# First projection and values of a hybrid encoder layer: scaled fp16 pairs for rounded-fp32 pairs, and values in 512 columns

## The chip, the core and the metric

The program runs on one core of a Trainium2 chip. The metric is the device time of one execution in microseconds; a version's time is the median of its runs. TensorE is called PE below, its weight loads PEld, VectorE DVE, ScalarE ACT, GpSimd POOL and SyncE SP. Hi and lo are the two halves of a pair that stands for one fp32 number: hi is the number in a shorter format, lo is what is left of it.

## What is computed

The layer works on 2048 tokens of 1024 features. The part that the change touches is its first line and what reads it:

```python
y = rmsnorm(h, norm_mix_g[l]) @ w_in[l]                 # (2048, 1024) @ (1024, 2560)
q = partial_rotary(y[..., 0:D_ATT].reshape(B, S, ATT_HEADS, HEAD_DIM))          # 512 columns
k = partial_rotary(y[..., D_ATT:2 * D_ATT].reshape(B, S, ATT_HEADS, HEAD_DIM))  # 512
v = y[..., 2 * D_ATT:3 * D_ATT].reshape(B, S, ATT_HEADS, HEAD_DIM)              # 512
att = dilated_sliding_attention(q, k, v).reshape(B, S, D_ATT)
c0 = 3 * D_ATT
conv = conformer_conv(y[..., c0:c0 + D_CONV], y[..., c0 + D_CONV:c0 + 2 * D_CONV],   # a, g
                      conv_w[l], conv_b[l], conv_ln_g[l], conv_ln_b[l])
h = h + jnp.concatenate([att, conv], axis=-1) @ w_out[l]
```

`conformer_conv` begins with `a * sigmoid(g)` and a convolution of 31 taps over the tokens. A cross-attention to 256 memory tokens and an MLP follow; the change doesn't touch them. The gain `norm_mix_g` lies around 5.7 here, and the weights are of the order of 1/32.

## The kernel before

**Layout and products.** The activations are kept feature-major: 8 tiles of 128 features (`KC`), 4 groups of 512 tokens (n = 0 to 3). Each product of the layer that needs fp32 accuracy is three matmuls (`mm3`, L201 to L204): hi by hi (L202), hi by lo and lo by hi (L203, L204), all in rounded fp32 (fp32r). A weight tile is 8 x 128 rows of 128 output columns. ACT makes its hi (L193), POOL or DVE its lo (L194), in `wsplit2`.

**Stages up to the first attention.** `setup0` and `setup` transpose the gains into `gv` and the convolution's weights into `cw` (times 0.5). `memory` projects the memory and forms two products of weights, which go to `ascr` and `bscr`; it uses the tiles of token groups 2 and 3 as scratch. Woven into it, `xprep` loads x, transposes it on PE (tile xt, L336), stores x^T to `xscr`, multiplies by gain and rms on DVE and splits the result into `XH_` (ACT) and `XL_` (POOL).

The projection follows as a row of units, one for each weight tile, run by `pipeline` (L494): the unit that computes is followed by one whose weights are being split and one whose weights are being loaded. The row is glu 0, glu 1 (each a unit g and a unit a, for token groups 0 and 1), eight units of keys and queries (`lin_qk`; kr and qr hold the rotary rows, gathered with strides), then glu 2, values 0, glu 3, values 1. Each tile of 512 tokens takes 24 matmuls into the PSUM tile `lin`. ACT takes the tanh of g, and DVE forms `u = (tanh + 1) * a`, which goes to `uscr`.

`lin_v` turns the operands round: a tile of 128 tokens of x is the stationary operand and 256 weight columns move, so a unit has 16 tiles of tokens of 24 matmuls each (tile v) into `vtok`, as an fp16 pair. `vscale` first works out a power of two for each value column (tile vsq: squares on ACT, sums on POOL and PE, the power on POOL and a bit mask on DVE). `lin_v` broadcasts it over the partitions (tile vbc, a transpose on PE) and multiplies the raw weights by it (L575). Its inverse, `vinv`, is applied after the attention. `edges` fills the first and last 256 rows of `vtok` from a tile of zeros, `zrow`, which is one of the two buffers of the tag raw.

**Beside it.** The convolution's 31 steps per tile (L219, DVE) are woven into the units. During the first attention, `rest` (L1118) weaves in glu 0 to 3 for token groups 2 and 3 in fine steps, each unit with its weights loaded and split again; then two tiles of `w_out` are fetched ahead.

**What sets the order.** Within each engine instructions run in the order in which the program's scheduler put them; it follows the order of the code and its own time line. Nearly all DMAs are issued by one queue, SP, in order, and one whose buffer isn't free yet holds those behind it. Raw weight tiles have two buffers, and so have their halves.

Of the kernel before, what the change touches and what calls it, by code (L numbers as in the profile page):

```python
# [10 lines left out]
F32 = mybir.dt.float32  # L11
# [10 lines left out]
P = 128  # L22
# [25 lines left out]
def hybrid_layer(ctx, tc, A, out):  # L48
# [12 lines left out]
    top.tile([P, 304], F32, name="tpad")  # L61
# [78 lines left out]
    cst.tile([P, 48], F32, name="cpad")  # L140
    lin = ExitStack()
# [7 lines left out]
    def setup():  # L149
# [14 lines left out]
        ACT.activation(cw.rearrange("p a b -> p (a b)"), pv[:, 64:192], AF.Copy, scale=0.5)  # L164

# [49 lines left out]
    def conv_unit(c, n, alloc, u):  # L215
        acc = alloc("acc", (P, 512), f"cacc{c}_{n}")
        DVE.tensor_scalar(acc, u[:, 0:512], cw[:, c, 0:1], gain("conv_b", c), op0=ALU.mult, op1=ALU.add)
        for t in range(1, CW):
            DVE.scalar_tensor_tensor(acc, u[:, t:t + 512], cw[:, c, t:t + 1], acc, op0=ALU.mult, op1=ALU.add)  # L219
            if t % 4 == 0:  # L220
                yield
# [62 lines left out]
    lp = pool("lin", stack=lin)  # L284
    xna.update({n: pool(f"x{n}", stack=early, side="right") for n in (0, 1)})
# [3 lines left out]
    def xpool(part, i, n, name, shape=(P, 2, 512), dtype=F32R):  # L289
        return xna[n].tile(list(shape), dtype, tag=f"x{part}{i}", name=name)  # L290
# [33 lines left out]
    def xprep(sp, n):  # L324
# [8 lines left out]
        for k in range(KC):  # L333
# [7 lines left out]
            DVE.scalar_tensor_tensor(xv, pt, gain("mix", k), rbs, op0=ALU.mult, op1=ALU.mult)  # L341
            ACT.copy(XH_[k, n], xv)
            POOL.tensor_tensor(XL_[k, n], xv, f(XH_[k, n]), op=ALU.subtract)
# [6 lines left out]
    def memory(sp):  # L350
        nat = [load_nat(sp, A["mem"][0, P * j:P * (j + 1), :], f"mn{j}") for j in range(2)]
        mh, ml = ([xpool(q, i, 3, f"m{q}{i}", (P, 4, NMEM)) for i in range(2)] for q in "hl")
# [22 lines left out]
        def wtiles(name, shape=(P, 8, P)):  # L375
            i = cnt[0] % 4
            cnt[0] += 1
            if i < 2:
                return [wp.tile(list(shape), dt, tag=t, name=f"m{t}_{name}", bufs=2)
                        for t, dt in (("raw", F32), ("whi", F32R), ("wlo", F32R))]  # L380
            return [xpool(q, j, 2, f"m{q}{j}_{name}", shape, dt)
                    for q, j, dt in (("h", i - 2, F32), ("h", i, F32R), ("l", i, F32R))]
# [21 lines left out]
        def ttiles(name):  # L404
            return [[xpool(q, 2 + i, 3, f"t{q}{name}{i}", (P, 4, NMEM)) for i in range(2)] for q in "hl"]
# [88 lines left out]
    def pipeline(*units):  # L494

        next(units[0])
        next(units[0])
        if len(units) > 1:
            next(units[1])
        for i, u in enumerate(units):  # L500
            if i + 1 < len(units):
                next(units[i + 1])
# [1303 lines left out]
```

## Time and profile before

| | |
|---|---|
| time, median of 3 runs | 2836.22 us (2830.67 to 2845.19) |
| profiled execution: time | 2833.89 us |
| profiled execution: span of the trace | 2832.1 us |
| mean granted clock of PE | 0.991 |
| matmuls in the trace | 15148 |
| bytes moved | 552.00 MB, 195 GB/s over the span |

The profile is one execution. Its span goes from the first to the last recorded instruction; 1.8 us of the execution lie outside it. Busy times are sums per engine over the span. In the views of groups a row has the count, the sum and the mean of one instruction, then the idle time of its engine just before them and what ended it. In a timeline a row has the start in us, the duration, the engine, the line, the operation, and output <- inputs with their shape. Matmuls are pipelined, so the duration of one is longer than the distance to the next. The chain of waits is read from top to bottom in order of time; a row has its start, its length and the work that ended last there.

### The profile page before, as it was taken

Reading aid. Unit: us, or ns where it says so; the run is one execution under the profiler, and the core shown is the slowest. Engines: PE = TensorE matmul, PEld = TensorE weight load, DVE = VectorE, ACT = ScalarE, POOL = GpSimd, SP = SyncE. Lnnn points to the kernel's source line nnn. Section 1 sums busy time; section 2 is a strip of 40 time slices with the busy share of each in tenths; the row PEclk is TensorE's granted clock in tenths of the full one; section 3 lists DMA queues with packets and bytes.
Section 4 is the critical chain, followed back from the end, with each engine's and each line's share of the span. In section 5 each row is a group of like instructions: output and inputs, shape, how many; then the busy total and the mean of one; then the engine's idle time right before and its main releaser. Section 6 shows DMA issues by size and latency. Waiting matters only on the chain.

```text
span 2832.1 us, 41590 instructions
## 1 busy us (share of the span) xinstructions
PE 2742.3 (97%) x15148; PEld 2304.1 (81%) x15148; DVE 1900.0 (67%) x3424; ACT 1234.4 (44%) x2140; POOL 571.3 (20%) x712
## 2 busy tenths in 40 slices
PE   8999999998899999999999999999999999999998
PEld 8878899877687888888878888887887788878877
DVE  6636545455689886668977488766475776666766
ACT  6633211465444434434454444454354444444435
POOL 1337321133103123310221202221010122200000
PEclk9999999999899999999999999999999999999999
DMA  8979844798735767776457867764534554484553
GB/s 279 318 160 236 196 128 138 182 247 221 206 118 153 226 211 218 238 238 202 144 171 228 264 194 228 240 224 147 178 119 130 171 201 160 171 294 160 171 182 105
DMA packets 609093, 552.00 MB, mean 195 GB/s; under 512 B 181221, under 2 KB 485401, under 8 KB 608888
## 3 DMA queue, kind: packets, MB, share of 16 engines
q1 hardware_dynamic: 550600, 462.30, 55.8%
q0 software_dynamic: 20336, 70.17, 6.5%
q10 hardware_dynamic: 37952, 16.88, 2.3%
q8 instruction: 119, 1.95, 0.3%
q14 instruction: 86, 0.70, 0.1%
HBM read 389.18 MB, written 160.06 MB: 194 GB/s over the span
## 4 chain that ended last, share of the span: by engine, by line
PE 76%; DMA 8%; DVE 5%; issue 5%; ACT 2%; SPq 1%; POOL 1%; POOLq 0%; ACTq 0%; DVEq 0%
PE b L1504 9%; PE dn L202 4%; PE dn L203 4%; PE dn L204 4%; PE up L202 4%; PE up L204 4%; PE up L203 4%; PE lin L202 4%; PE lin L204 3%; PE lin L203 3%; PE s L1010 2%; PE pt L797 2%; PE xs L202 1%; SPq L57 1%; PE xs L203 1%
## 5 line engine op out<-in xcount | busy, mean ns | idle before, releaser
L219 DVE SCALAR_TENSOR_TENSOR cacc<-cu,cw,cacc 128x512 f32<-128x512 f32 x480 | 392.4, 819 | 6.4
L791 ACT ACTIVATE sm<-sm,o 128x256 f32<-128x256 f32 (+1 forms) x384 | 161.5, 467 | 113.8 <-DVE o L790 113.4
L202 PE MATMUL up<-mh,whi_u 128*128 128x512 f32 x512 | 202.3, 395 | 0.0
L202 PE MATMUL dn<-hhh,whi_d 128*128 128x512 f32 x512 | 199.8, 400 | 1.6 <-DVE h L1356 0.9
L203 PE MATMUL dn<-hhl,whi_d 128*128 128x512 f32 x512 | 200.1, 393 | 0.2 <-DVE hhl L1342 0.2
L204 PE MATMUL up<-mh,wlo_u 128*128 128x512 f32 x512 | 200.0, 391 | 0.0
L203 PE MATMUL up<-ml,whi_u 128*128 128x512 f32 x512 | 199.6, 390 | 0.0
L204 PE MATMUL dn<-hhh,wlo_d 128*128 128x512 f32 x512 | 198.9, 391 | 0.0
L790 DVE CUSTOM_DVE_ANT_0 sm<-s,mask 128x256 f32<-128x256 f32 (+1 forms) x384 | 129.0, 375 | 59.5 <-PE s L1010 31.8
L801 DVE TENSOR_TENSOR pl<-pt,ph 128x512 f16<-128x512 f32 x160 | 109.3, 686 | 44.3 <-ACT ph L800 43.4
L180 POOL TENSOR_TENSOR nr<-st_v,mhalf 128x4 f32<-128x4 f32 x12 | 13.3, 1104 | 603.3 <-DVE st_v L176 603.3
L1356 DVE TENSOR_TENSOR h<-h,dn 128x512 f32<-128x512 f32 x128 | 86.2, 683 | 65.7 <-PE dn L204 65.0
L800 ACT CAST ph<-pt 128x512 f16<-128x512 f32 x160 | 92.1, 577 | 82.4 <-PE pt L797 80.1
L204 PEld LDWEIGHTS up<-mh,wlo_u 128*128 128x128 f32 x512 | 96.1, 188 | 20.5
L204 PEld LDWEIGHTS dn<-hhh,wlo_d 128*128 128x128 f32 x512 | 96.2, 188 | 20.4
L203 PEld LDWEIGHTS dn<-hhl,whi_d 128*128 128x128 f32 x512 | 96.4, 188 | 18.5 <-DVE hhl L1342 0.9
L202 PEld LDWEIGHTS dn<-hhh,whi_d 128*128 128x128 f32 x512 | 95.4, 188 | 19.7 <-DVE h L1356 1.5
L203 PEld LDWEIGHTS up<-ml,whi_u 128*128 128x128 f32 x512 | 96.2, 188 | 18.6
L202 PEld LDWEIGHTS up<-mh,whi_u 128*128 128x128 f32 x512 | 96.2, 188 | 18.3
L203 PE MATMUL o<-catl,whi_o 128*128 128x512 f32 x256 | 102.6, 401 | 2.3 <-DMA catl<-catl 2.3
L202 PE MATMUL o<-cath,whi_o 128*128 128x512 f32 x256 | 103.1, 404 | 1.5 <-ACT cath L959 0.8
L204 PE MATMUL o<-cath,wlo_o 128*128 128x512 f32 x256 | 102.2, 400 | 0.8 <-DVE wlo_o L194 0.8
(568 smaller groups left out, 8361.9 us busy)
## 6 DMA issues: line engine op xcount, KB each, us to landing
raw_u<-in_w_up_dram SPq DMA_DIRECT2D x64, 512.0 KB
raw_d<-in_w_down_dram SPq DMA_DIRECT2D x64, 512.0 KB
raw_o<-in_w_out_dram SPq DMA_DIRECT2D x32, 512.0 KB
raw_a<-ascr SPq DMA_DIRECT2D x32, 512.0 KB
raw_b<-bscr SPq DMA_DIRECT2D x32, 512.0 KB
lou<-wlo_u POOLq DMA_DIRECT2D x32, 512.0 KB, 5.5
lod<-wlo_d POOLq DMA_DIRECT2D x32, 512.0 KB, 5.4
wlo_u<-lou SPq DMA_DIRECT2D x32, 512.0 KB
```

Source lines behind the costliest of these rows:

```text
L202: PE.matmul(o, lh, rh, start=first, stop=False)
L203: PE.matmul(o, lh, rl, start=False, stop=False)
L204: last["pe"] = PE.matmul(o, ll, rh, start=False, stop=end)
L219: DVE.scalar_tensor_tensor(acc, u[:, t:t + 512], cw[:, c, t:t + 1], acc, op0=ALU.mult, op1=ALU.add)
L790: last["dve"] = DVE.tensor_tensor_reduce(dst, so, mask[:, 256 * m:256 * m + nk], 1.0, 3e38, ALU.add, ALU.min, mn)
L791: last["act"] = ACT.activation(dst, dst, AF.Exp, bias=mn, scale=-1.0)
L797: last["pe"] = PE.transpose(pt[:, j, :], sm[:, j, :], ident)
L800: ACT.copy(ph, pt)
L801: DVE.tensor_tensor(pl, pt, ph, op=ALU.subtract)
L1010: last["pe"] = PE.matmul(o, q_[x][:, qs], kv, start=x == 0, stop=x == 1)
L1356: last["dve"] = DVE.tensor_tensor(hs[m], hs[m], pt, op=ALU.add)
L1504: PE.matmul(o, w[i][:, k, :], Y[b][q][k], start=first and k + x == 0, stop=k == 3 and x == 2, skip_group_check=not first)
```

## The change

1. **Types.** The x tiles `XH_`, `XL_` and the weights' halves in the projection are fp16 in place of fp32r. `mm3` itself is the same. In the row of PE, an fp16 matmul has a weight load (LDWEIGHTS) as a row of its own.
2. **Scales.** fp16 has a short range of exponents, so power-of-two scales from the data are put in. `setup` finds one from the largest squared gain: `gmix` is the gain times it, `back` its inverse (also times 0.5, -0.125 and 1024). Each of the 16 weight tiles gets one from the sum of its squares (`wscale`): squares and sum on ACT, a one-column matmul on PE (`sqs_*`), maximum on DVE, power on POOL, bit mask, reciprocal and product on DVE. `scaled_split` multiplies the tile by it (ACT), then hi (ACT) and lo (POOL). The second pass over the glu weights uses the kept scales.
3. **Scales taken out again** where a result was read anyway: in the tanh's scale, in the convolution's weights (`cwu` = `cw` times the scale), in the evacuation of q and k, in `vinv` and in the evacuation of the values.
4. **Values.** One unit with 512 weight columns and 16 tiles of tokens, in place of two units with 256. Its four raw tiles keep the tag raw and come in two pairs. The row of units ends glu 2, glu 3, values.
5. **Pipeline.** The units have four stages before they compute (load, squares, scale, split). The next one is split, the second next squared, the third next loaded. Raw tiles of the projection have three buffers under their own tag.
6. **Room.** `memory` gets a pool of its own in place of the x tiles, two unused paddings are gone, and `ahead` yields twice more.

The core of the diff:

```diff
+        g8 = gv[:, GV["mix"]:GV["mix"] + 8]
+        DVE.tensor_tensor(gmix, g8, g8, op=ALU.mult)
+        DVE.tensor_reduce(top_[:, 0:1], gmix, axis=AX.X, op=ALU.max)
+        bcast_rows(pg, top_[:, 0:1], 1)
+        DVE.tensor_reduce(top_[:, 1:2], pg[:, 0:P], axis=AX.X, op=ALU.max)
+        DVE.tensor_scalar(top_[:, 2:3], top_[:, 1:2], 2.0 ** -20, 1e-30, op0=ALU.mult, op1=ALU.max)
+        pow2_below(top_[:, 4:5], top_[:, 2:3], top_[:, 3:4])
...
+    def pow2_below(dst, v, t):
+        POOL.tensor_tensor(t, v, mhalf, op=ALU.pow)
+        DVE.tensor_scalar(dst.bitcast(I32), t.bitcast(I32), 0x7F800000, None, op0=ALU.bitwise_and)
+    def wscale(raw, key, factor):
+        if key not in kept_scale:
...
+            ACT.activation(junk, raw, AF.Square, accum_out=v[:, 0:1])
+            yield
+            PE.matmul(pc[:, 0:1], small, v[:, 0:1], start=True, stop=True)
+            DVE.tensor_scalar(v[:, 1:2], pc[:, 0:1], 1e-30, None, op0=ALU.max)
+            pow2_below(c, v[:, 1:2], v[:, 2:3])
+            DVE.reciprocal(v[:, 3:4], c)
+            DVE.tensor_scalar(e, v[:, 3:4], back[:, factor:factor + 1], None, op0=ALU.mult)
+            yield
...
+    def scaled_split(raw, c, hi, lo, eng):
+        ACT.activation(raw, raw, AF.Copy, scale=c)
+        ACT.copy(hi, raw)
+        eng.tensor_tensor(lo, raw, hi, op=ALU.subtract)
+    def wlin(kind, name):
+        return lp.tile([P, 8, P], F32 if kind == "raw" else F16, tag="l" + kind, name=f"l{kind}_{name}",
+                       bufs=3 if kind == "raw" else 2)
...
-            wh, wl = wsplit2(wp, raw, f"{x}{c}{ns[0]}", lo_eng=POOL)
+            yield from wscale(raw, f"{x}{c}", 1 if x == "g" else 0)
+            scaled_split(raw, sc, wh, wl, POOL)
...
-                    ACT.activation(sig[n], pt, AF.Tanh, scale=0.5)
+                    ACT.activation(sig[n], pt, AF.Tanh, scale=e)
...
-            for k in range(KC):
-                w = sq[k // 4][:, k % 4]
-                ACT.activation(w, w, AF.Square, scale=gain("mix", k))
+            for q in range(2):
+                ACT.activation(sq[q], sq[q], AF.Square)
...
+        load(0)
+        load(1)
+        yield
+        split(0)
+        split(1)
+        load(2)
+        load(3)
+        yield
+        yield
+        split(2)
+        split(3)
+        yield
+        for t in range(4 * NG):
...
-            st = lbv.tile([P, 4, VW], F16, tag="vst", name=f"vst{g}_{t}", bufs=6)
+            st = lbv.tile([P, 8, VW], F16, tag="vst", name=f"vst_{t}", bufs=4)
...
-            ACT.copy(st[:, :, 0:HD], p3)
-            last["dve"] = DVE.tensor_tensor(st[:, :, HD + 2:VW], p3, st[:, :, 0:HD], op=ALU.subtract)
+            ACT.activation(st[:, :, 0:HD], p3, AF.Copy, scale=2.0 ** -10)
+            last["dve"] = DVE.scalar_tensor_tensor(st[:, :, HD + 2:VW], p3, 2.0 ** -10, st[:, :, 0:HD], op0=ALU.mult,
+                                                   op1=ALU.subtract)
...
-        steps = pipeline(*units, *glu(2, early01), lin_v(0, alln), *glu(3, early01), lin_v(1, alln))
+        steps = pipeline(*units, *glu(2, early01), *glu(3, early01), lin_v())
```

Three places in the rows of the engines show what this moves.

The first is TensorE at the start of the values. Before, these rows end the unit a of glu 3 (tile lin, weights whi_a and wlo_a) and begin the second unit of values (v1_0 to v1_3 are its first four tiles of tokens, wvh10 and wvl10 its weights, xh0_0 and xl0_0 the first tile of x):

```order
L203 MATMUL lin_4699<-xl3_1_1666,whi_a30_4597 128x512
L204 MATMUL lin_4699<-xh3_1_1665,wlo_a30_4598 128x512
L202 MATMUL v1_0_4727<-wvh10_4659,xh0_0_578 128x256
L202 MATMUL v1_1_4757<-wvh10_4659,xh0_0_578 128x256
L202 MATMUL v1_2_4794<-wvh10_4659,xh0_0_578 128x256
L202 MATMUL v1_3_4824<-wvh10_4659,xh0_0_578 128x256
L203 MATMUL v1_0_4727<-wvl10_4660,xh0_0_578 128x256
L204 MATMUL v1_0_4727<-wvh10_4659,xl0_0_579 128x256
```

After the change, at the same place (the weights are one tile, wvh and wvl, and the matmuls of `mm3` stand at L255 to L257):

```order
L257 MATMUL lin_4380<-xh3_1_1687,lwlo_a30_4262 128x512
L255 LDWEIGHTS xh0_0_600
L255 MATMUL v_0_4412<-wvh_4191,xh0_0_600 128x512
L255 LDWEIGHTS xh0_0_600
L255 MATMUL v_1_4442<-wvh_4191,xh0_0_600 128x512
L255 LDWEIGHTS xh0_0_600
L255 MATMUL v_2_4480<-wvh_4191,xh0_0_600 128x512
L255 LDWEIGHTS xh0_0_600
L255 MATMUL v_3_4510<-wvh_4191,xh0_0_600 128x512
L255 LDWEIGHTS xh0_1_1681
L255 MATMUL v_4_4548<-wvh_4191,xh0_1_1681 128x512
L256 LDWEIGHTS xh0_0_600
```

Five matmuls by wvh, in place of four, now stand ahead of the first one by wvl, which follows in the next row. Between the last transpose vbc3 and these rows stand 18 matmuls of lin; before, 23 stood between vbc11 and v1_0.

The second place is TensorE near the end of the unit k0 (tile lin of its last token group, xh_3). Before, the unit q0 follows without anything in between:

```order
L202 MATMUL lin<-xh_3_2221,whi_k_2675 128x512
L203 MATMUL lin<-xl_3_2222,whi_k_2675 128x512
L204 MATMUL lin<-xh_3_2221,wlo_k_2676 128x512
L202 MATMUL lin<-xh_0_578,whi_q_2878 128x512
L203 MATMUL lin<-xl_0_579,whi_q_2878 128x512
```

After, the sum of squares of a later key tile (sqv_k) is broadcast there through the constant tile small:

```order
L257 LDWEIGHTS lwlo_k_2775
L257 MATMUL lin<-xh_3_2301,lwlo_k_2775 128x512
L198 MATMUL sqs_k_3038<-sqv_k_2996,small 128x1
L255 LDWEIGHTS lwhi_k_2774
L255 MATMUL lin<-xh_3_2301,lwhi_k_2774 128x512
L256 LDWEIGHTS lwhi_k_2774
L256 MATMUL lin<-xl_3_2302,lwhi_k_2774 128x512
L257 LDWEIGHTS lwlo_k_2775
L257 MATMUL lin<-xh_3_2301,lwlo_k_2775 128x512
L255 LDWEIGHTS lwhi_q_2990
```

One matmul that needs the load and the squares of a weight tile two units on now stands inside the unit's last tile.

The third place is the queue SP around the loads for the unit kr. Before, with raw_k the load for k0, rope_* the rotary tables, xts_* the tiles of x^T on their way to xscr, u_* the products of the glu:

```order
L57 DMA rope_kr_2329<-in_rope_dram 128x512
L57 DMA rope_kr_2331<-in_rope_dram 128x512
L57 DMA xscr_75<-xts_0_2304 128x512
L57 DMA xscr_76<-xts_1_2316 128x512
L57 DMA vtok<-zrow 256x1x1040 x2
L57 DMA uscr_72<-u_0_2367 128x512
L57 DMA raw_k_2499<-in_w_in_dram 128x8x48 x2
```

After, with lraw_* the projection's raw tiles, raw_v_* those of the values and eb_* tiles of the memory's second product on their way to bscr:

```order
L57 DMA lraw_g_1943<-in_w_in_dram 128x8x128
L57 DMA vtok<-zrow 256x1x1040
L57 DMA bscr<-eb_1745 128x4x128
L57 DMA bscr<-eb_1755 128x4x128
L57 DMA bscr<-eb_1765 128x4x128
L57 DMA vtok<-zrow 256x1x1040
L57 DMA lraw_a_1954<-in_w_in_dram 128x8x128
L57 DMA bscr<-eb_1775 128x4x128
L57 DMA raw_v_4193<-in_w_in_dram 128x8x128
L57 DMA raw_v_4195<-in_w_in_dram 128x8x128
L57 DMA lraw_kr<-in_w_in_dram 128x8x16 x7
```

The two stores of zero rows and the first two raw tiles of the values moved ahead of the loads for kr, among the stores of the memory's product; the mask of the attention (in_masks) follows a few rows later, also ahead of where it was.

More of the change, by code (lines that the diff above doesn't have):

```diff
@@ L284, in hybrid_layer @@
     lp = pool("lin", stack=lin)
+    small = lp.tile([P, P], F32, name="small")
+    DVE.memset(small, 2.0 ** -30)
     xna.update({n: pool(f"x{n}", stack=early, side="right") for n in (0, 1)})
@@ L769, in hybrid_layer @@
             next(steps)
[L770 to L772 removed]
+        weave(islice(steps, 4), (conv0, 1))
         weave(steps, (conv0, 2.2))
```

153 lines of the change are left out of this document (92 added, 61 removed).

## Prediction

> **What bounds the kernel now.** I read the page's list of engines first, then a table of busy time by stretch of the program, then who TensorE waits for in those stretches, and last the timeline for the pitch (start to start) of its matmuls.
>
> ```profile
> span 2832.1 us, 41590 instructions
> PE 2742.3 (97%) x15148; PEld 2304.1 (81%) x15148; DVE 1900.0 (67%) x3424; ACT 1234.4 (44%) x2140; POOL 571.3 (20%) x712
> ```
>
> TensorE (PE) is busy 97% of the span. That average says little of one stage, so the next table, from the windows view, gives the stretches that the change touches: start-up with the memory's projections (0 to 128), the first projection and the values (128 to 530), and the first attention, into which the projection's last third is woven (530 to 725).
>
> ```profile
> core 0: us, PE busy (x) PEld busy (x) DVE busy (x) ACT busy (x) POOL busy (x), PEclk, DMA share, GB/s
> 0.00:128.00 128.00, 115.81 (x845) 108.65 (x846) 92.18 (x147) 84.93 (x169) 32.58 (x29) 0.99 0.94 297
> 128.00:190.00 62.00, 62.00 (x295) 51.47 (x294) 20.41 (x32) 21.87 (x38) 25.19 (x18) 1.00 0.76 160
> 190.00:202.00 12.00, 6.23 (x25) 4.91 (x24) 3.30 (x5) 2.13 (x4) 3.40 (x3) 0.72 0.94 270
> 202.00:530.00 328.00, 328.00 (x1828) 287.65 (x1827) 167.04 (x241) 79.86 (x144) 122.83 (x129) 1.00 0.70 178
> 530.00:725.00 195.00, 176.64 (x1620) 155.64 (x1618) 118.00 (x481) 123.49 (x295) 53.13 (x75) 0.97 0.87 220
> ```
>
> From 202 to 530 us TensorE is never idle while VectorE (DVE) is busy for 51% and ScalarE (ACT) for 24% of the time. In this stretch the time is the number of matmuls times their pitch, and extra work on the other engines is free as long as TensorE doesn't come to wait for it. The one hole before it is at 190 to 202 us. In the attention TensorE is idle for 18.4 us of 195.
>
> **The change part by part.** Matmul durations in the tables overlap, so I take the pitch from first and last rows of unbroken runs.
>
> ```profile
> 260.08 0.39 PE L202 MATMUL lin<-xh,whi_q 128*128 128x512 f32 x1
> ...
> 266.88 0.39 PE L202 MATMUL lin<-xh,whi_q 128*128 128x512 f32 x1
> ```
> ```profile
> 400.01 0.28 PE L202 MATMUL v<-wvh,xh 128*128 128x256 f32 x1
> ...
> 403.97 0.28 PE L202 MATMUL v<-wvh,xh 128*128 128x256 f32 x1
> ```
> ```profile
> 562.90 0.19 PE L805 MATMUL opt<-v,ph 128*128 128x65 f16 x1
> ...
> 563.23 0.19 PE L807 MATMUL opt<-v,pl 128*128 128x65 f16 x1
> ```
>
> A rounded-fp32 matmul of 512 columns takes 6.80 us / 30 = 226.7 ns, one of 256 columns 3.96 / 33 = 120.0 ns. The difference gives 106.7 / 256 = 0.417 ns a column, and what is left over is 13.3 ns for each matmul whatever its width. The fp16 matmuls of the attention (two of 65 columns and one of 64, so 64.7) follow at 0.33 / 11 = 30.0 ns. Their columns take 27.0 of that, so only 3.0 ns are left over, although each has its own weight load. No fp16 matmul of 512 columns is in this trace. Its pitch lies between 213.4 (columns alone) and 226.7 (the same width in rounded fp32). I take the row of the same type: 213.4 + 3.0 = 216.4.
>
> The Trainium skill, page "TensorE: Matmul & The Clock Gate", section "Back-to-back issue gap", gives columns / 2.4 + 2.5 ns, that is 215.7 ns. By it the PE term below would be 26.3 us. The rounded-fp32 rows here are 11 ns above that formula, which doesn't tell types apart.
>
> The numbers of matmuls stand in the view of the tile lin and in the group of the values:
>
> ```profile
> L202 PE MATMUL lin<-xh,whi_g x128: 389/389/486, 127.9 to 685.9; 128*128 128x512 f32 x128
> L202 PE MATMUL lin<-xh,whi_a x128: 388/389/776, 142.0 to 718.8; 128*128 128x512 f32 x128
> L202 PE MATMUL lin<-xh,whi_k x96: 389/389/486, 231.4 to 340.7; 128*128 128x512 f32 x96
> L202 PE MATMUL lin<-xh,whi_q x96: 389/389/486, 253.3 to 362.9; 128*128 128x512 f32 x96
> L202 PE MATMUL lin<-xh,whi_kr x32: 387/389/628, 177.0 to 208.6; 128*128 128x512 f32 x32
> L202 PE MATMUL lin<-xh,whi_qr x32: 389/389/389, 209.3 to 230.3; 128*128 128x512 f32 x32
> ```
> ```profile
> L202 PE MATMUL v<-wvh,xh 128*128 128x256 f32 x256 | 71.5, 283 | 0.0
> ```
>
> They sum to 512 at L202 and as many at L203 and L204: 1536 matmuls of 512 columns. 1536 x 10.3 ns = **15.8 us**. The values are 768 x 120.0 ns = 92.2 us now and become 384 of twice the width, 384 x 216.4 = 83.1 us: **9.1 us**. Together 24.9 us. With 213.4 it would be 30.7, with 226.7 it would be 5.1.
>
> The rows for the costs (lines view by shape, and TensorE's waits in 530 to 725):
>
> ```profile
> L193 ACT CAST whi_a<-raw_a 128x1024 fp32r<-128x1024 f32 x12 | 12.6, 1049 | 39.5 <-PE lin L203 14.3 <-DMA raw_a<-in_w_in_dram 11.1 <-issue 9.3
> L542 ACT ACTIVATE vsq<-vsq,gv 128x128 f32<-128x128 f32 x32 | 9.9, 389 | 3.6 <-DMA qfar<-sth_q 2.1 <-DMA vsq<-in_w_in_dram 1.4
> L194 POOL TENSOR_TENSOR wlo_a<-raw_a,whi_a 128x1024 fp32r<-128x1024 f32 x8 | 19.2, 2396 | 33.2 <-ACT whi_a L193 33.2
> L554 POOL TENSOR_TENSOR vs<-vs,mhalf 128x1 f32<-128x1 f32 x4 | 2.2, 562 | 0.0
> L553 DVE TENSOR_SCALAR vs<-vss 128x1 f32<-128x1 f32 x4 | 0.6, 149 | 0.0
> L575 DVE TENSOR_TENSOR raw_v<-raw_v,vbc 128x1024 f32<-128x1024 f32 x4 | 4.9, 1219 | 16.1 <-PE vbc L188 16.1
> L551 PE MATMUL vss<-ones,vsq 128*128 128x1 f32 x16 | 2.0, 228 | 0.0
> ```
> ```profile
> PE opt L807 <- DVE pl L801: 13.4, 15, 4.7
> PE opt L805 <- ACT ph L800: 3.0, 3, 1.2
> ```
>
> - **Scales of the weights.** Each of the 16 weight tiles of the projection gets a pass of squares on ACT (1.05 us by L193), a one-column matmul on TensorE, four small DVE operations (0.15 us each) and one power on POOL (0.56 us). Each of the 24 splits gets one more pass on ACT. ACT: 40 x 1.05 = 42 us, less the finer squares of the values (32 x 0.39 = 12.4 now, 8 passes after). DVE: 16 x 0.6 = 10 us; POOL 9 us. In 128 to 530 all of it lies beside TensorE, on engines that are idle for at least half of that time. What isn't beside TensorE are its own 16 one-column matmuls and the gain's transpose: 17 x 228 ns = 3.9 us at most, 0 at least. Neighbours overlap, so I take **2.0 us**.
> - **Attention.** 8 units x 2 tiles x 24 = 384 of the 1536 matmuls are woven into the attention, worth 4.0 us there. TensorE waits there for pl and ph, that is for DVE and ACT, and ACT gets 8 more passes (8.4 us) in one queue with the exponentials. If nothing covers them, the 4.0 us go and up to 8.4 more are lost; if all is covered, the 4.0 stay. I take half of the 4.0 back: **2.0 us**.
> - **Start of the values.** By the order of the rows, 18 + 5 matmuls (5.0 us) stand between the last vbc transpose and the first use of wvl. The chain in between is DVE 1.22 + ACT 1.05 + POOL 2.40 = 4.7 us. Before, it was 23 matmuls of 226.7 ns and 4 of 120.0 (5.7 us). A convolution step on DVE ahead of it (0.8 us) is now enough to hold TensorE: 0 to 3 us. The gain's scale in start-up puts one round of PE, DVE and POOL (1 to 2 us) ahead of the weights' subtractions on DVE. I take **1 us** for both.
> - **Fp16 outputs of POOL's and ACT's splits.** No POOL subtraction with fp16 is in the trace. If it took twice as long (2.4 us more for a tile), it would still be hidden by the 48 matmuls of a unit (10.4 us). 0.
> - **Loads moved on SP.** The zero rows of vtok, two value tiles and the mask go ahead of the loads for kr, and the raw tiles get a third buffer. What such a move does is shown by the hole at 190 us, in the chain of waits:
>
> ```profile
> 173.28 12.33 DMA vtok<-zrow
> ...
> 190.90 5.44 DMA xscr<-xts
> ...
> 197.94 1.08 PE xt L336 x4
> ```
>
> The weight load behind the zero rows waits 12.33 us for their buffer, SP issues in order, so the stores of x come late, DVE waits for their buffer and TensorE for DVE. It costs 12.00 - 6.23 = 5.8 us of idleness and, at a granted clock of 0.72, about 12 x 0.28 = 3.4 us: 9.2 us. Afterwards it is a value tile that waits for the same buffer, some 45 us earlier, again ahead of stores of x. I leave the 9.2 us in the sum; both other ends, gone and doubled, are rivals.
>
> Sum: -24.9 + 2.0 + 2.0 + 1.0 = -19.9 us. The profiled execution took 2833.89 us, 2.3 below the median of the three runs (2836.22). 2833.9 - 19.9 = **2814.0 us**.
>
> **The rivals.**
>
> A. *Fp16 doesn't shorten the pitch*: the 13.3 ns belong to any new weights of 128 columns, and only the values gain. 2833.9 - 5.1 + 5.0 = 2834 us. Against it: 3.0 ns are left over in the fp16 rows, with new weights each time. Chance 0.05.
>
> B. *The scale's matmul holds TensorE's queue* (slower). Until now a weight tile is needed on TensorE only at its unit's start, two units after its load was issued. Now its sum of squares stands in TensorE's row about one unit and a tile after the load, and everything behind it waits if the load or ACT is late.
>
> ```profile
> ACT whi_a L193 <- DMA raw_a<-in_w_in_dram: 11.1, 2, 5.6
> ```
>
> Twice in 128 to 530, ACT waited 5.6 us for a weight's landing. A glu tile on TensorE is 24 x 216.4 ns = 5.2 us, so such a lateness reaches TensorE as 0.4 us, and as 2.8 us when a POOL subtraction (2.4) stands ahead of the power. At 2.8 us for 16 tiles it is 45 us: 2814 + 45 = 2859 us. It turns the gain into nothing at 1.2 us for each tile. Against it: two waits in 400 us are few, and the DMA share from 202 to 530 is 0.70. Chance 0.09.
>
> C. *The weight loads are exposed*. The fp16 loads are instructions of their own in the row, 1920 of them.
>
> ```profile
> L805 PEld LDWEIGHTS <-ph 128*128 128x128 f16 x640 | 60.5, 97 | 22.7 <-issue 14.4 <-ACT ph L800 4.2 <-ACT sm L791 1.6
> ```
>
> If each waited for the matmul ahead of it, 1920 x 97 ns = 186 us would come on top: 3000 us. Against it: at a pitch of 30.0 ns a load of 97 ns can only lie beside matmuls. Chance 0.01. The Trainium skill's same page, under "The mechanism" of its Part 3, says that loads overlap running matmuls only where the row groups differ; by that rule C would come out, and the attention's full-height fp16 rows speak against it.
>
> D. *The hole at 190 us goes*, since the loads are no longer behind the zero rows: 2814 - 9 = 2805 us. Chance 0.15.
>
> E. *A second hole of that kind*, since 1 MB of zero rows, 1 MB of values and the mask now come where stores of x and of the memory's products are due: 2814 + 9 = 2823 us. Chance 0.12.
>
> **How the numbers follow.** The forecast, 2814 with a few us to either side, has 0.58; A 0.05, B 0.09, C 0.01, D 0.15, E 0.12. The range 2800 to 2830 takes in the forecast, D and E and leaves out 0.15; its ends are the pitch's lower bound with D, and A or E with a lost attention. A measurement of this kernel tells about 0.5% from no change, 14 us: faster means under 2822. The forecast and D are faster (0.73, less 0.02 for forecasts that come out near the line): 0.71. A and E are the same, with those 0.02 and a little of B: 0.20. The rest is slower: 0.09.
>
> **What would show it.** Right: matmuls of lin and v start 215 to 217 ns apart; the rows from the first lin to the end of the values are some 20 us shorter; no wait of TensorE there over 1 us except one for xt or at the first v. Wrong: a pitch near 227 (A); waits of PE at sqs or right behind it (B); idle stretches ended by loads (C); in 530 to 725, waits for ph and pl that grow by more than 4 us.

## The result and the profile after

The change makes the kernel slower: 2859.49 us (median of 7 runs, 2852.43 to 2874.24) against 2837.3 us before (7 runs). The ratio is 1.0083, 95% interval 1.0057 to 1.0109, which is some 24 us; the medians lie 22 us apart. The forecast was 2814. The profiled execution after took 2868.5 us, 9 above its median; a second profile of the same kernel (e_again, 2863.32 us) is set beside it below, so that one execution isn't taken for the rule. The one profile of before took 2833.89 us, 3 below the median, so the spans compared here lie 35 and 29 us apart, more than the medians do.

The shorter matmuls are there. The timeline of TensorE, first and last row of an unbroken run of lin and of v:

```profile
260.05 0.38 PE L255 MATMUL lin<-xh,lwhi_k 128*128 128x512 f16 x1
...
267.17 0.38 PE L255 MATMUL lin<-xh,lwhi_k 128*128 128x512 f16 x1
...
439.87 0.38 PE L255 MATMUL v<-wvh,xh 128*128 128x512 f16 x1
...
446.13 0.38 PE L255 MATMUL v<-wvh,xh 128*128 128x512 f16 x1
```

33 matmuls in 7.12 us and 29 in 6.26 us: 215.8 ns each, where 226.7 was the pitch before and 216.4 the forecast. So the 1536 matmuls of lin save 16.7 us and the values 9.3. The Trainium skill, page "TensorE: Matmul & The Clock Gate", section "Back-to-back issue gap", has 512 / 2.4 + 2.5 = 215.8 ns, and calls that the gap of an isolated matmul; for a stream of weight loads and matmuls of 512 columns it gives about 131 ns. The fp16 rows here are such a stream, and they agree with the first figure and not with the second. The rounded-fp32 rows of before (226.7) agree with neither.

Where this went is read from the same landmarks in each trace. The groups of the tiles lin, s and o give when the unit k0 starts, when the first attention starts and when it is over (in each row the first and the last start stand behind the three durations):

```profile
L255 PE MATMUL lin<-xh,lwhi_k x96: 376/379/379, 254.2 to 360.6; 128*128 128x512 f16 x96
```
```profile
L960 PE MATMUL s<-k,qh x128: 277/282/775, 540.0 to 739.6; 128*128 128x256 f32 x128
```
```profile
L255 PE MATMUL o<-cath,whi_o x256: 387/389/796, 750.2 to 2116.5; 128*128 128x512 f32 x128
```

| us of the trace | before | change | change, e_again | e_nowait | e_fix_late |
|---|---|---|---|---|---|
| k0 starts | 231.4 | 254.2 | 255.8 | 236.7 | 233.0 |
| from there to the attention | 294.3 | 285.8 | 288.2 | 285.6 | 276.9 |
| first attention | 198.1 | 210.2 | 202.5 | 206.9 | 200.5 |
| from there to the end | 2108.3 | 2116.5 | 2115.0 | 2114.8 | 2113.1 |
| span | 2832.1 | 2866.7 | 2861.5 | 2844.0 | 2823.5 |

The middle stretch got shorter. In it run 768 of the matmuls of lin and all of the values, worth 8.4 + 9.3 = 17.7 us by the pitch. The change shows 6 to 8.5 us of that, e_fix_late (section 5) 17.4. The start-up lost over 20 us, the attention 4 to 12. The start-up by the windows view, before and after, up to 123 us and from there to k0:

```profile
0.00:123.00 123.00, 110.81 (x822) 104.79 (x823) 89.99 (x144) 80.18 (x160) 28.87 (x27) 0.99 0.93 295
123.00:231.40 108.40, 102.63 (x473) 84.60 (x471) 36.29 (x52) 43.06 (x73) 54.22 (x43) 0.97 0.86 203
```
```profile
0.00:123.00 123.00, 107.73 (x788) 101.23 (x788) 81.97 (x148) 73.60 (x151) 26.56 (x27) 0.99 0.93 285
123.00:254.20 131.20, 114.43 (x523) 59.77 (x523) 51.28 (x92) 72.37 (x104) 55.09 (x49) 0.92 0.81 191
```

Behind 123 us TensorE was idle for 5.8 us before the change and is idle for 16.8 now, and its granted clock there fell from 0.97 to 0.92. ACT has 72.4 us of work in place of 43.1, and yet it isn't its work that fills the time. Its waits from 120 to 260 us:

```profile
ACT sqj_kr L195 <- DMA lraw_kr<-in_w_in_dram: 8.9, 1, 8.9
ACT sqj_a L195 <- DMA lraw_a<-in_w_in_dram: 8.8, 1, 8.8
ACT sqj_qr L195 <- DMA xn<-in_x_dram: 8.2, 1, 8.2
```

Three times the pass of squares stands at the head of ACT's queue for 8 to 9 us until a load has landed. (The third row names a load of x, xn; SP issued it right behind those of lraw_qr, which this pass reads.) The chain of waits shows what stands behind it, and what the loads themselves waited for:

```profile
128.78 0.91 ACT sqj_a L195
...
138.00 7.89 DMA vtok<-zrow
...
157.46 3.67 DMA lraw_kr<-in_w_in_dram
161.24 1.15 ACT sqj_kr L195 x2
162.39 0.57 ACT eb L528
162.97 0.58 ACT sig L598
```

Behind the squares for kr come the evacuations eb of the memory's product and sig of the glu. The zero rows of vtok now take 7.9 us ahead of the loads for kr; before, they took 12.3 us behind them. Before the change ACT came to the weights of kr only when they were there. The views of the tiles raw_kr and lraw_kr, before and after (SPq is the queue that issues the loads):

```profile
L57 SPq DMA_DIRECT2D raw_kr<-in_w_in_dram x8: 373/578/877, 145.6 to 150.5; - x8
L624 ACT CAST whi_kr<-raw_kr x2: 1197/1228/1259, 166.0 to 167.0; 128x512 fp32r<-128x512 f32 x2
```
```profile
L57 SPq DMA_DIRECT2D lraw_kr<-in_w_in_dram x8: 582/894/1922, 147.6 to 157.5; - x8
L195 ACT ACTIVATE sqj_kr<-lraw_kr x1: 1056/1056/1056, 161.2 to 161.2; 128x1024 bf16<-128x1024 f32 x1
L710 ACT CAST lwhi_kr<-lraw_kr x2: 2452/2595/2738, 203.5 to 205.5; 128x512 f16<-128x512 f32 x2
```

Before, the last of these loads was issued at 150.5 us and the cast started at 166.0. Now the last is issued at 157.5, and ACT has stood at the squares since 152.4. The last row shows something else: the cast of the rotary weights takes 2.6 us to fp16, where it took 1.2 to rounded fp32. TensorE waits for it:

```profile
PE lin L255 <- ACT lwhi_kr L710: 3.3, 1, 3.3
```

### The profile page after: what moved, and what is told of

It is laid out like the page before. It is cut to its first block, busy times and chain, and to the rows that moved or that the text cites. A ratio compares the mean times of both kernels' runs of the same rounds, so it can differ in the third digit from the quotient of the medians.

```text
span 2866.7 us, 40890 instructions
## 1 busy us (share of the span) xinstructions
PE 2744.5 (96%) x14797; PEld 2135.2 (74%) x14797; DVE 1913.0 (67%) x3491; ACT 1277.9 (45%) x2156; POOL 567.1 (20%) x713
## 4 chain that ended last, share of the span: by engine, by line
PE 69%; DMA 10%; DVE 7%; issue 5%; ACT 5%; POOL 2%; SPq 2%; ACTq 0%; DVEq 0%; POOLq 0%
PE b L1593 6%; PE dn L255 4%; PE dn L256 4%; PE dn L257 4%; PE up L255 4%; PE up L256 3%; PE up L257 3%; PE lin L255 2%; PE lin L256 2%; PE lin L257 2%; SPq L57 2%; PE s L1097 2%; PE pt L884 2%; DMA raw_ub<-in_w_up_dram 2%; PE x L255 1%
## 5 line engine op out<-in xcount | busy, mean ns | idle before, releaser
L272 DVE SCALAR_TENSOR_TENSOR cacc<-cu,cwu,cacc 128x512 f32<-128x512 f32 x480 | 393.1, 820 | 6.4
L255 PE MATMUL dn<-hhh,whi_d 128*128 128x512 f32 x512 | 200.1, 401 | 2.5 <-ACT hhh L1430 1.5
L255 PE MATMUL up<-mh,whi_u 128*128 128x512 f32 x512 | 202.3, 395 | 0.0
L257 PE MATMUL up<-mh,wlo_u 128*128 128x512 f32 x512 | 200.0, 391 | 0.0
L256 PE MATMUL up<-ml,whi_u 128*128 128x512 f32 x512 | 199.7, 390 | 0.0
L257 PE MATMUL dn<-hhh,wlo_d 128*128 128x512 f32 x512 | 199.6, 393 | 0.0
L884 PE MATMUL pt<-ident,sm 128*128 128x128 f32 x640 | 102.9, 280 | 9.4 <-ACT sm L878 6.2
L257 PEld LDWEIGHTS dn<-hhh,wlo_d 128*128 128x128 f32 x512 | 96.5, 189 | 20.6
L257 PEld LDWEIGHTS up<-mh,wlo_u 128*128 128x128 f32 x512 | 96.1, 188 | 20.5
L255 PEld LDWEIGHTS dn<-hhh,whi_d 128*128 128x128 f32 x512 | 95.5, 188 | 20.6 <-ACT hhh L1430 2.1
L255 PEld LDWEIGHTS up<-mh,whi_u 128*128 128x128 f32 x512 | 96.2, 188 | 18.3
L255 PE MATMUL o<-cath,whi_o 128*128 128x512 f32 x256 | 103.4, 405 | 6.4 <-DMA cath<-cath 4.9
```

The source lines that it names most:

```text
L255: PE.matmul(o, lh, rh, start=first, stop=False)
L256: PE.matmul(o, lh, rl, start=False, stop=False)
L257: last["pe"] = PE.matmul(o, ll, rh, start=False, stop=end)
L272: DVE.scalar_tensor_tensor(acc, u[:, t:t + 512], cwu[:, c, t:t + 1], acc, op0=ALU.mult, op1=ALU.add)
L884: last["pe"] = PE.transpose(pt[:, j, :], sm[:, j, :], ident)
```

## The experiments

Each edit is made to the changed kernel. Ratios are to the kernel before, whose own median lay between 2837.8 and 2838.8 us in these runs.

**1. The chain of the scales.** Three runs. The first replaces it by a constant:

```diff
-            ACT.activation(junk, raw, AF.Square, accum_out=v[:, 0:1])
-            yield
-            pc = ps("c", f"sqs_{key}")
...
-            DVE.tensor_scalar(e, v[:, 3:4], back[:, factor:factor + 1], None, op0=ALU.mult)
+            yield
+            c, e = 2.0 ** 11, wscl[:, i + 1:i + 2]
+            DVE.tensor_scalar(e, back[:, factor:factor + 1], 2.0 ** -11, None, op0=ALU.mult)
```

> The changed kernel with the constant 2^11 as scale of every weight tile of the projection (the value that these weights give), so no squares on ACT, no one-column matmul, no power on POOL and no small operations for it; the scaling pass, the splits and all else stay. Theory 1, the chain that works out the scales holds the queues of ACT and TensorE in start-up: the unit k0, which now begins at 254 us of the trace, begins before 235, and the time falls by 15 to 25 us from 2859 to about 2840. Theory 2, the zero rows, value tiles and mask that were moved ahead in SP's queue cost the start-up: k0 begins after 248 and the time falls by 2 to 5 us at most. Theory 3, the loss lies in the first attention, by the extra pass on ACT: k0 may begin a few us earlier, the attention stays as long as it is.

Measured: 2847.62 us, ratio 1.0035 (1.0021 to 1.0048); k0 at 244.1. That is less than theory 1 asked for. ACT's waits give a likely reason: the scaling pass now stands where the squares stood:

```profile
ACT lraw_kr L697 <- DMA lraw_kr<-in_w_in_dram: 9.8, 1, 9.8
ACT lraw_qr L697 <- DMA uscr<-u: 8.7, 1, 8.7
ACT lraw_q L203 <- DMA lraw_q<-in_w_in_dram: 8.2, 2, 7.0
ACT lraw_a L203 <- DMA lraw_a<-in_w_in_dram: 8.1, 1, 8.1
```

So work and wait had to be separated. The second run keeps the work and takes away what it waits for:

```diff
-            ACT.activation(junk, raw, AF.Square, accum_out=v[:, 0:1])
+            ACT.activation(junk, flat, AF.Square, accum_out=v[:, 0:1])
...
+    flat = lp.tile([P, 8, P], BF16, name="flat")
+    DVE.memset(flat, 2.0 ** -5)
```

> The changed kernel with the squares taken of a constant tile (all 2^-5, whose sum gives the same scale 2^11) in place of the raw weights. The whole chain stays: squares on ACT, one-column matmul, power, mask, reciprocal, product; only it waits for no load any more. Theory 1a, the cost is the wait for the loads on in-order queues: the time comes to 2845 to 2850 as with constant scales, k0 begins at 243 to 247 us. Theory 1b, the cost is the chain's work (16 passes of 1.05 us on ACT in start-up and its hops): the time stays at 2856 or above and k0 begins after 251.

Measured: 2841.32 us, ratio 1.0007 (0.9993 to 1.0021), 18 us below the change and no slower than the kernel before; k0 at 236.7. All of the chain's work is still there; the scaling and the casts still wait for their loads. ACT's longest wait for a load between 120 and 240 us is now one of 6.1 us:

```profile
ACT lraw_a L211 <- DMA lraw_a<-in_w_in_dram: 6.1, 1, 6.1
...
ACT junk L369 <- DMA xn<-in_x_dram: 2.2, 1, 2.2
```

Theory 1b falls. Theory 1a holds in its direction; k0 comes 6 us earlier and the time is 4 us lower than it gave. One thing came with it: the loads of the last tokens of x (xn), which stood behind those for kr and qr in SP's queue, stand ahead of them here. The third run holds SP's order row by row and only puts the squares further back in ACT's queue ("a" is the last evacuation on ACT that was traced ahead):

```diff
+            with ExitStack() as st:
+                after(st, "a")
+                ACT.activation(junk, raw, AF.Square, accum_out=v[:, 0:1])
```

> The changed kernel with each pass of squares put behind the last operation on ACT that evacuates a result (the tanh of a glu tile, the cast of an x tile, the evacuation of a key or query tile) that is traced ahead of it. SP's order is that of the changed kernel row by row; what moves is the place of the squares in ACT's queue, and of a few one-column matmuls in TensorE's. Theory 1a: the three waits of 8 to 9 us that ACT spends on sqj_a, sqj_kr and sqj_qr shrink to less than half of their 26 us, k0 begins at 245 to 250, and the time falls by 4 to 8 us to about 2853. Rival, it is the order of the loads in SP (x behind kr and qr) that sets the start-up: k0 stays within 3 us of 255.

Measured: 2857.84 us, ratio 1.0063 (1.0041 to 1.0084), k0 at 247.4. The place in ACT's queue alone is worth 7 to 8 us at k0. The intervals of this run and of the change overlap, so the time itself doesn't settle it, and the 2853 us of theory 1a weren't reached. The other 10 us or so of e_nowait's gain at k0 are not taken apart: the loads come in another order there, and here one wait for a weight is left, besides those for x:

```profile
ACT junk L369 <- DMA xn<-in_x_dram: 10.5, 3, 7.1
ACT sqj_a L197 <- DMA lraw_a<-in_w_in_dram: 8.5, 1, 8.5
```

**2. The transfers that moved ahead.** The zero rows, the value tiles and the mask get an edge behind later DMAs on SP ("sp" is the last one traced ahead), alone and with constant scales:

```diff
+    with ExitStack() as st:
+        after(st, "sp")
+        edges()
```

> The changed kernel with only three transfers moved back in SP's queue: the zero rows of vtok behind the last store of x^T, the first two value tiles behind the loads of glu 3, the mask behind the last two value tiles. Theory 2 (2.8 MB ahead of the loads for kr and x): the 7.9 us wait behind the zero rows and about 10 us of transfer time go, k0 begins near 240 in place of 254, and the time falls by 10 to 15 us to about 2847. Theory 1 (the chain of the scales): k0 begins within 4 us of 254, and the time falls by less than 5.

> Both edits together: constant 2^11 for the scales of the weights, and zero rows, value tiles and mask moved back in SP's queue. If the two causes are separate, the gains add and the time is near 2830; if one is all, it equals that one's run within 4 us; k0 begins at 225 to 230, as the shorter matmuls ahead of it would have it (231 before, less 384 matmuls of 11 ns).

Measured: 2862.14 us (ratio 1.0094, 1.0067 to 1.0121) and 2860.56 us (1.0078, 1.0059 to 1.0096); k0 at 245.0 and 239.9. At k0 theory 2 has the direction, 9 and 4 us earlier, but not all it asked for: with both edits k0 was expected at 225 to 230. The time didn't follow. My edit made two longer waits on TensorE further on. In e_late:

```profile
PE v L257 <- ACT wvh L652: 6.3, 1, 6.3
PE vss L625 <- POOL vsq L618: 5.1, 1, 5.1
```

The zero rows now collide with the loads for vscale, and the one-column matmul vss holds TensorE; and the value tiles come so late that the cast wvh does (3.6 us of wait there in the change). With constant scales these are 8.1 us for wvh and 7.0 (two waits) for vss. So these two runs tell nothing of the total; section 5 repeats the edit with the attention's prefetch out of the way.

**3. The start of the values.** In the change ACT's timeline around the last cast of the value weights reads:

```profile
422.97 1.15 ACT L211 ACTIVATE lraw_a<-lraw_a,wscl 128x1024 f32<-128x1024 f32 x1 [5.16 <-DMA lraw_a<-in_w_in_dram]
426.41 1.04 ACT L246 CAST whi_o<-raw_o 128x1024 fp32r<-128x1024 f32 x1 [2.29 <-DMA raw_o<-in_w_out_dram]
427.36 1.04 ACT L650 CAST wvh<-raw_v 128x1024 f16<-128x1024 f32 x1
```

The cast's input was ready at 422.8 (DVE's L648). It waits 4.6 us behind two weights that are fetched ahead for the attention and aren't there yet. The edit puts those behind it:

```diff
-            ACT.copy(wh[:, :, es], raws[e])
+            last["wv"] = ACT.copy(wh[:, :, es], raws[e])
...
-        rest = pinned(pipeline(*(u for c in range(4) for u in glu(c, (2, 3), True)), ahead(0), ahead(1)), "pe")
+        rest = pinned(pipeline(*(u for c in range(4) for u in glu(c, (2, 3), True)), ahead(0), ahead(1)), "pe", "wv")
```

> The changed kernel with one edit of order: the ACT operations of the weights fetched ahead for the attention (second pass of the glu tiles, and w_out) come behind the last cast of the value weights in ACT's queue. Theory 5, the hole at the start of the values (7.9 us from vbc to v, 8.1 us lost with the half clock behind it) is the wait of these operations for their loads, in front of the cast wvh: v begins at most 5 us behind the last vbc, no wait of TensorE there is over 1.5 us, and the time falls by 5 to 8 us to about 2853. Rival, the chain of four operations itself is too long for the 18 matmuls that cover it: a wait of 3 us or more stays and the time falls by less than 3.

Measured: 2858.18 us, ratio 1.0065 (1.0046 to 1.0084). v starts 4.0 us behind the last vbc (7.9 in the change), the only wait left there is

```profile
PE v L255 <- DVE u L601: 1.6, 1, 1.6
```

and from the last vbc to the attention it takes 113.1 us in place of 119.4. The mechanism is shown, at 6.3 us of the trace. In the time it doesn't stand out of the scatter of these runs.

**4. The attention's extra pass, and the unchanged kernel again.**

```diff
-        ACT.activation(raw, raw, AF.Copy, scale=c)
-        ACT.copy(hi, raw)
-        eng.tensor_tensor(lo, raw, hi, op=ALU.subtract)
+        ACT.activation(hi, raw, AF.Copy, scale=c)
+        DVE.scalar_tensor_tensor(lo, raw, c, hi, op0=ALU.mult, op1=ALU.subtract)
```

> The changed kernel with the scaling done inside the split: hi comes from one ACT pass with the scale, lo from one DVE operation (raw times scale, less hi), so the separate ACT pass and POOL's subtraction are gone for the 22 splits that are not the rotary rows. Theory 3 (the extra ACT passes in the attention cost its 12 us): the stretch from the first s to the first o, 210 us now, shortens by 6 to 10 us, and so does the time. Theories 1 and 2: the stretch keeps its length within 3 us, the start-up gains 1 to 3 us by the shorter chain.

> The changed kernel once more, unedited, for a second profile: how far do the stretches of one program differ from execution to execution? The first profile took 2868.5 us, 9 above the median of its runs. Theory 1: the start of k0 (254.2 us) and of the attention (540.0) stay within 4 us, since the waits there come from the order of the queues, and the attention's 210 us within 3. Theory 4, a good part of what the first profile shows is accident of one execution (landing times of DMAs): k0 begins 5 us or more earlier and the attention takes 203 to 205 us, as in the four experiments before.

Measured: e_direct 2856.14 us, ratio 1.0061 (1.0040 to 1.0081), attention 200.5 us; e_again 2863.32 us, k0 at 255.8 and the attention from 544.0, 202.5 us long. The start-up's loss is the same in both profiles of the change. Of the attention's 210 us, 8 were an accident of the first one. The other experiments allow a better comparison: in the nine profiles with the extra pass the attention takes 202.5 to 210.2 us, 203.8 in the middle; in the six without it (and without POOL's subtraction) 195.1 to 200.5, 199.7 in the middle. So the pass costs about 4 us there, not 10, and theory 3 is a small part of where the time went.

**5. Everything together.** Two edits to memory's buffers were tried with constant scales first: four pairs and four raw tiles as before the change.

```diff
-            if i % 5 < 2:
+            if i % 4 < 2:
...
-            if i % 3 < 2:
+            if i % 4 < 2:
```

> The run with constant scales, and besides four pairs of hi and lo tiles and four raw tiles for the memory's projections, as before the change, in place of three and five (the projection's raw tiles have two buffers then). Theory 6, the memory's third pair lost makes the products of weights wait for their splits (two pairs are in use, one is free, so the second split of the next head comes late): the first lin begins at 129 to 131 in place of 136 us, k0 at 235 to 239 in place of 244, and the time falls by 4 to 8 us from 2848 to about 2841. Rival, the 5 to 9 us come from the gain's scale in setup or from the extra transfers: the first lin stays after 134.

Measured: 2850.31 us, ratio 1.0043 (1.0026 to 1.0060), k0 at 244.9 as without it. The first lin, which theory 6 put at 129 to 131 us, comes at 148.4, 12 us later than without the edit, and k0 doesn't follow it. Theory 6 falls.

> All of these together: constant scales, four pairs for the memory, the attention's prefetch behind the value weights, and the split with the scale inside it. It is the change without its side effects, so what is left should be the shorter matmuls. If the causes add: from 2848, 6 for the memory, 6 for the values and 4 for the attention give 2832, some 6 below the kernel before; with the whole predicted gain of the matmuls (24.9 us) it would be near 2815. If the start-up is bound by transfers, whatever the order, it stays at 2840.

> The repaired kernel with fixed scales (e_fix), and besides the zero rows, value tiles and mask moved back in SP's queue as in e_late. Theory 7, early bytes: start-up is bound by transfers, and 2.9 MB at some 250 GB/s are 11 us; k0 begins at 230 to 234 us in place of 239, and the time falls by 3 to 8 us to about 2821. Rival, the value tiles that come late hold the start of the values (10 to 12 us from vbc to v in the late runs), now without the attention's prefetch in front of them: k0 gains 4 us and the values give back as much, and the time stays within 4 us of 2826.

Measured: 2826.47 us, ratio 0.9947 (0.9927 to 0.9968), and 2821.35 us, ratio 0.9936 (0.9913 to 0.9958): both faster than the kernel before, though by less than the 24.9 us that the matmuls were to give. With the prefetch out of the way, the later transfers bring k0 from 239.2 to 233.0, as theory 7 said; the time falls by some 5 us, with intervals that overlap. In e_fix_late TensorE waits three times in all from 123 to 430 us:

```profile
PE vss L616 <- POOL vsq L609: 2.4, 1, 2.4
PE xt L384 <- DVE xv L389: 1.8, 1, 1.8
PE v L249 <- POOL wvl L644: 0.5, 1, 0.5
```

**6. Scales from the data.** The first try keeps 16 scales, each worked out one unit ahead and behind the last evacuation:

```diff
-            to(i + 2, 2)
             to(i + 3, 1)
-            for _ in u:
-                yield
-                to(i + 2, 3)
+            yield from u
```

> Real scales from the data, with three repairs: the weights' whole preparation happens one unit ahead, with the squares behind the last evacuation in ACT's queue; the split takes the scale in its own two passes; the attention's prefetch comes behind the value weights. If the causes found so far are the main ones: start-up 5 us, values 6, attention 4 less than the 2859 of the change, 2842 to 2846, still not below the kernel before. If the wait in ACT's queue was all of the start-up's loss it comes to 2830 to 2835.

Measured: 2864.9 us, ratio 1.0090 (1.0065 to 1.0116), a miss. ACT's waits for weights are gone from the top of its list, but TensorE now comes to the sums before they are there:

```profile
PE sqs_a L200 <- ACT sqj_a L197: 5.9, 1, 5.9
PE xt L392 <- DVE xv L397: 5.6, 3, 3.7
PE lin L256 <- ACT lwhi_kr L708: 4.2, 1, 4.2
PE sqs_q L200 <- DVE vs L623: 2.6, 1, 2.6
```

The second has one scale for all tiles, from the squares of the first:

```diff
-        if key not in kept_scale:
+        if not kept_scale:
...
+        elif key not in kept_scale:
+            yield
+            kept_scale[key] = wscl[:, 0:1], wscl[:, 1 + factor:2 + factor]
+            yield
```

> One scale for all weight tiles, worked out from the squares of the first (g of glu 0) as in the change, in place of 16; with the split that takes the scale in its two passes, the prefetch behind the value weights, and the zero rows, value tiles and mask moved back in SP's queue; memory's buffers as in the change. 15 of 16 waits for a load in front of ACT's queue are gone, the scales still come from the data. Theory 1a: within 5 us of the kernel with fixed scales (2821), so 2818 to 2827, some 15 us below the kernel before. Rival, the memory's four pairs were needed for that: 2828 or more, with the first lin later than 140 us.

Measured: 2827.51 us, ratio 0.9963 (0.9946 to 0.9979), k0 at 235.5. With 15 of the 16 passes of squares gone and the scale still from the data, the kernel is faster than before by 10 us, half a us above what theory 1a gave. Its first lin comes at 131.4, so the memory's four pairs weren't needed.

**7. The gain's scale**, fixed at 2^7 on top of e_fix_late:

```diff
-        top_ = t2("gtop", F32, (P, 8))
...
+        DVE.tensor_scalar(gmix, g8, 2.0 ** 7, None, op0=ALU.mult)
```

> The kernel of the last run with fixed scales (e_fix_late), and the gain's scale fixed too (2^7, the value that these gains give): the eight operations and the transpose for it in start-up are gone. What is still open is the memory's stage: its last matmul pxv comes at 115 us there and at 105.8 before the change. Theory 8, the gain's chain delays the first splits: pxv ends at 106 to 109, the first lin and k0 come 4 to 7 us earlier, and the time falls to about 2816. Rival, it isn't the chain but the order and the rate of the transfers: pxv ends after 112 and the time stays within 4 us of 2821.

Measured: 2821.86 us, ratio 0.9946 (0.9931 to 0.9961); pxv ends at 116.7. Theory 8 falls: the gain's chain costs nothing that shows.

## Why the prediction was wrong

- **The pitch** (-24.9 us): right, 215.8 ns for 216.4, for lin and for the values, and in the stretch where nothing else got in its way (k0 to the attention in e_fix_late) its gain arrives. Rivals A and C are out: 1920 weight loads with new weights lie beside the matmuls. The rule of the Trainium skill that was set against it (page "TensorE: Matmul & The Clock Gate", Part 3, "The mechanism": loads overlap running matmuls only where the row groups differ) isn't borne out by these rows, whose loads and matmuls use all 128 rows. The same section also lets a load into the background weight buffer go ahead; whether that is what happens here no row shows. The other sign that was named didn't come: from the first lin to the last v it takes 380.9 us in place of 371.8, not 20 less.
- **"In 128 to 530 all of it lies beside TensorE, on engines that are idle for at least half of that time"**: this is the step that failed. It counted the chain's durations (42 us on ACT) against ACT's idle time. With all that work, and squares that wait for no load, the kernel is at 1.0007. What costs is that an idle engine can still be held: a pass of squares that stands in ACT's row before its weight has landed, with the evacuations eb and sig and the casts of x behind it. That was 26 us of waits for ACT, and 17 to 19 us at k0 together with the order of the loads that came with them. The length of such a wait isn't its price. In e_fix_late ACT stands for 8.8 us in front of the scaling of kr, and TensorE has two waits, 4.2 us in all, from 123 us to k0:

```profile
ACT lraw_kr L701 <- DMA uscr<-u: 8.8, 1, 8.8
```

- **Rival B** named the mechanism (an operation for the scale that holds an in-order queue until its load lands) and gave 2859 us. The figure agrees by chance: it put the wait on TensorE's queue, where the change waits 1.8 us at one sqs, and at 2.8 us for each of 16 tiles. It was three long waits on ACT. Moved one unit later the same chain does hold TensorE (e_best, 5.9 us). I gave it 0.09 because ACT had waited for weights only twice before. In the code the squares stand one unit behind the load, as the casts did; in ACT's row the casts of kr came 15.5 us behind the last issue of their loads, and the squares ahead of it.
- **Fp16 outputs** (0): right for POOL, wrong for the rotary weights, whose split takes twice as long on ACT (1.2 to 2.6 us) and on DVE (1.2 to 2.4). In both profiles of the change TensorE waits 3.3 us for the second of ACT's casts. In e_nowait and e_fix_late, where these casts start at 179 and 174 us in place of 204, it doesn't. What this alone is worth no run shows.
- **Loads moved on SP**: the hole of 9.2 us was left in the sum, with "gone" and "doubled" as rivals D and E. E was nearer. The 9.2 us count idle time a second time in the low clock; with the slow matmuls behind it (about 1.8 us lost from 197.9 to 201.7) the hole is nearer 7.6. Moving the transfers back is worth 9 us at k0 alone and 6 in the repaired kernel.
- **Start of the values** (0 to 3 us, 1 taken with the gain): 6.3 us. The chain of DVE, ACT and POOL was sized rightly. What else stands between its links in ACT's queue, the prefetch for the attention, was not looked up.
- **Attention** (-2 us): +4 by the second profile. The extra pass is about 4 of it; so the gain of the shorter matmuls there, another 4 us, doesn't show either, and why stays open.
- **Memory's room** was costed at nothing without a reason. TensorE does 3 us less work up to 123 us in the change (110.81 and 107.73), and pxv ends 6 us later. Neither the pairs (e_const_mem4) nor the gain (e_fl_gain) is the cause. It stays open. So do 3 to 16 us from the attention to the end (all profiles of changed kernels), in code that the change doesn't touch and against a single profile of before.

## What to carry to other kernels

An operation that waits for a transfer costs its queue its wait, not its duration, and costs the kernel what the bounding engine misses meanwhile; when work is added to an engine with idle time, look up where each new operation stands in that engine's row, what it waits for and whose results stand behind it. Before a gain on the bounding engine is booked, ask in which stage that engine is the bound: in this start-up even the best run reached k0 no earlier (233.0 us) than the kernel before (231.4), with 384 shorter matmuls ahead of it. An edit that takes a load out of one collision is judged by the time only when the next user of the same queue has been looked at too.

## What the runs showed of the hardware

A hole on TensorE costs more than its length. After the 4.4 us wait at 184 us the fp16 matmuls follow at 427 ns until 193 us, double the 215.8 ns of the undisturbed rows; the granted clock from 188.4 to 193.2 us is 0.51. Before the change the rounded-fp32 ones followed at some 425 ns until 201.7 us, behind the hole of 5.8 us. The rows around the change of pace:

```profile
188.39 0.48 PE L391 MATMUL xt<-ident,xn 128*128 128x128 f32 x1 [4.40 <-DMA xn<-in_x_dram]
...
190.37 0.63 PE L255 MATMUL lin<-xh,lwhi_a 128*128 128x512 f16 x1
190.79 0.63 PE L256 MATMUL lin<-xl,lwhi_a 128*128 128x512 f16 x1
...
193.21 0.38 PE L256 MATMUL lin<-xl,lwhi_a 128*128 128x512 f16 x1
193.43 0.38 PE L257 MATMUL lin<-xh,lwlo_a 128*128 128x512 f16 x1
```

In the change four holes of 2.1 to 4.4 us (they end at 151, 176, 188 and 208 us) each have 3.4 to 5.3 us at half pace behind them; the one hole of 5.8 us before has 3.8. So several short holes were dearer here than one long one.

POOL's subtraction, of which the prediction asked whether fp16 might double it, takes 2.13 to 2.28 us to fp16 (groups of lwlo) in place of 2.39 to 2.55. What did double are the rotary weights' cast on ACT and subtraction on DVE, 128x512 elements written in another order than they are read: 1.2 us each to rounded fp32, 2.4 to 2.6 to fp16. Their input is scaled now, and hi and lo have another type; nothing else in these operations changed.
